# An accumulating transfer for one weight sum, spaced output pieces, early copies of z and start loads from another queue

## The chip, the cores and the metric

One core of a Trainium2 chip runs the kernel; there are no other cores in the program. The metric is device time in microseconds (us) of one execution. Engines are named as in the profile: PE (TensorE), PEld (its weight loads), DVE (VectorE), ACT (ScalarE), POOL (GpSimd), SP (SyncE, which issues most of the transfers). Each engine works through its own instructions in order.

## The reference, cut to what matters

Sixteen learned tokens are put ahead of 512 rows of x, and two layers follow. In each, one wide projection feeds a gated short convolution and a retention branch of four heads; both outputs are gated, summed, projected and normed.

```python
for l in range(DEPTH):                       # DEPTH = 2, D_MODEL = 1024, T = 528
    xn = _rmsnorm(h, pre_norm_g[l])
    proj = xn @ w_in[l] + b_in[l]            # 1024 x 12288
    c_h, c_b, c_c, c_z, r_q, r_k, r_v, r_z, g_a, g_b = jnp.split(proj, split_at, axis=-1)
    y_a = _short_conv_branch(c_h, c_b, c_c, c_z, conv_w[l], conv_b[l], w_conv_out[l])
    y_b = _retention_branch(r_q, r_k, r_v, r_z, ret_gn_g[l], w_ret_out[l])
    y = jax.nn.sigmoid(g_a) * y_a + jax.nn.sigmoid(g_b) * y_b
    y = y @ w_o[l]
    h = h + _rmsnorm(y, post_norm_g[l])
return h[:, N_META:]
```

The convolution branch is `gb * (conv_b + taps of gc * h) * silu(z) @ w_out`. The retention branch rotates q and k, forms decayed scores, multiplies v with them, norms each head's output, multiplies by `silu(z)` and ends in `@ w_out` (four heads of 512 columns).

## The kernel before

Everything is float32. Each matrix is split into a high part (ACT's cast to fp32r) and a low part (DVE's subtraction), by `split`, L139 to L141, and a product takes three matmul passes: high by high, low by high, high by low. Token positions lie along the free axis, 264 to a matmul in the first layer and about 256 to 264 in the second.

The projection goes in blocks of 256 columns, 86 of them as a `Group` (L288). A group treats its 1024 x 256 weight block as 2 x 2 blocks B11, B12, B21, B22 and computes the product with seven block products in place of eight (Winograd's form), each `mul` of 12 matmuls; Xh and Xl hold the blocks A11, A12, A22 of the input and four sums S1 to S4. The weight side needs sums of blocks too. `Group.load` (L299 to L306) fetches three raw tiles of 128 x 1024 by SP: j = 0 with w_0 in the first half and w_1 in the second, j = 1 with w_3 in the second, j = 2 with w_2 in the first and w_1 in the second. The halves of 512 columns are separate transfers of 256 KB. `halves(j)` then adds the first half onto the second (L311, DVE, for j = 0 and for j = 2; for j = 2 this is B22 + B12) and splits the tile (L140 ACT, L141 DVE). `sums` forms two further sums on DVE (L318 from the second half of tile 0 and the first half of tile 2; L319), and `last` splits the fourth tile.

`run` (L331 to L368) issues the seven products into the banks pb, pc and pa. After the first product ACT copies the bank, with the bias, into the shared bank pa (L339), onto which a later product accumulates; `put` evicts the others by ACT (L329). The last product is kept back (`end`) and is issued within the next unit of work.

The order of work is set by three things. `later(delay, fn)` puts small steps into a queue of ticks, and `tick` comes after each product. `load` and `prep` queue transfers and splits, and `pump` issues them as raw slots (six, NSRC) and split pairs (four, NPAIR) come free. The tile scheduler then places the instructions of each engine in a fixed order, and steps under `tc.high_priority()` are preferred in it.

The places that the change touches:

- `conv_group` (L549 to L604) makes the four groups of a convolution block. The last head's four output pieces, `RetOut` (L526; its matmuls are L248), are added with the second convolution block (L938 to L942): two after its third group and two after its fourth. Each piece multiplies that head's normed outputs `yr` with a weight pair and adds onto YB (L546). The blocks 2 and 3 follow (`add_conv`).
- At the start SP issues, in turn, pieces of x (L996) and of the weights of the first K and Q blocks (L1000). ACT's queue has gpre's transfer (L120), an activation table load and the write to `ident` (L981); then come the first prescales and casts, and PE's first projection matmuls (L672).
- The first projections run before the norm's factor R is known. `raw_out` (L1032) copies their results from the banks, and `with_r` (L1035 multiply on DVE, L1036 activation on ACT) applies R and the bias later; for the four tiles of z the activation is Silu (L1073), ahead of the splits of A11, A12, A22 (L1076).
- POOL runs a few memsets of `Slo` (L872) and the `pow` of each norm (L379).

Of the kernel before, what the change touches and what calls it, by code (L numbers as in the profile page):

```python
# [14 lines left out]
AF = mybir.ActivationFunctionType  # L15
ALU = mybir.AluOpType
# [40 lines left out]
def trunk(ctx: ExitStack, tc: tile.TileContext, xT, w_in, binT, w_co, w_ro, w_o, gpre, gpost,  # L57
# [230 lines left out]
    class Group:  # L288
# [10 lines left out]
        def load(self, j, w):  # L299

            t = self.raw[j] = src()
            if j == 1:
                nc.sync.dma_start(t[:, 512:], w[:, 3, :])
                return
            nc.sync.dma_start(t[:, 0:512], w[:, j, :])
            nc.sync.dma_start(t[:, 512:], w[:, 1, :])  # L306

        def halves(self, j):
            if j != 1:
                r = self.raw[j]  # L310
                nc.vector.tensor_tensor(r[:, 512:], r[:, 512:], r[:, 0:512], op=ALU.add)  # L311
# [238 lines left out]
    def conv_group(l, i2, res):  # L550
# [44 lines left out]
        def c_b(ts):  # L595
# [3 lines left out]
            for s in range(2):  # L599
                later(s, lambda s=s: product(s))  # L600
                later(1 + s, lambda s=s: res.append(halves_of(cs, ts[s])))

        return [Group(l, C_H + i2 * 256, I_CONV[l], c_h), Group(l, C_C + i2 * 256, I_CONV[l], c_c),
                Group(l, C_Z + i2 * 256, I_Q[l], c_z, AF.Silu), Group(l, C_B + i2 * 256, I_Q[l], c_b)]  # L604

# [222 lines left out]
    for l in range(DEPTH):  # L828
# [96 lines left out]
        for h in range(1, H):  # L925
# [9 lines left out]
            for b in range(2):  # L935
                add(Group(l, R_Z + h * DV + b * 256, I_Q[l],
                          lambda ts, d=d, h=h, l=l, yr=yrs[h]: z_done(ts, d, h, l, yr), AF.Silu))
        for n, g in enumerate(conv_group(l, 1, conv)):  # L938
            add(g)
            if n >= 2:  # L940
                for q in (2 * n - 4, 2 * n - 3):
                    add(RetOut(l, H - 1, q), yrs[H - 1])  # L942
        add_conv(2)
        add_conv(3)

# [49 lines left out]
    for ks in (slice(0, 1), slice(1, 2), slice(2, 4), slice(4, 6), slice(6, 8)):  # L995
# [3 lines left out]
        for g, c in enumerate((R_K, R_Q)):  # L999
            nc.sync.dma_start(entry[g][j]["raw"].rearrange("p (n k c) -> p n k c", n=2, k=4)[:, :, kk, :],  # L1000
                              w_in[0, c // 256][:, 2 * j:2 * j + 2, :].rearrange("p n (k c) -> p n k c", k=4)[:, :, kk, :])
    for k in range(KD):
# [28 lines left out]
    def raw_out(d, o, m):  # L1031
        nc.scalar.copy(d, o)  # L1032

# [37 lines left out]
    zt = hd["z"][0].ts + hd["z"][1].ts  # L1071
    for n in range(4):
        with_r(zt[n], R_Z // P + n, AF.Silu)  # L1073
    for b, half, j in ((A11, 0, 0), (A12, 0, 4), (A22, 1, 4)):
        for kk in range(0, 4, 2):
            split(Xh[:, b, kk:kk + 2], Xl[:, b, kk:kk + 2], YH[:, j + kk:j + kk + 2, half, :])  # L1076
    later(14, lambda: z_done(zt, jobs[0][0]["hd"], 0, 0, jobs[0]["yrs"][0], (), 13, 8))

# [236 lines left out]
```

## Time and profile before

| | us |
|---|---|
| median of 3 runs | 1537.32 (1536.90 to 1538.46) |
| the profiled execution | 1536.42 |
| its span | 1534.3 |
| PE busy | 1522.3 (99%) |
| PEld busy | 1478.8 (96%) |
| DVE busy | 1172.6 (76%) |
| ACT busy | 916.0 (60%) |
| POOL busy | 27.1 (2%) |
| mean granted clock of PE | 0.999 |

The span is the profile's own time from the first to the last instruction; the execution's time has 2.1 us around it. Busy time of PE is modelled at the ends of matmuls, so neighbouring matmuls overlap in it: in a steady stretch starts are 0.12 us apart and each matmul shows as 0.28 us. A loss is best read from the distance of two starts. Idle time of an engine other than PE costs nothing by itself; it matters where PE waits for that engine.

### The profile page before, as it was taken

The page shows a single profiled execution, that of the slowest core. Times are in us where ns is not written, and L with a number is a line of the kernel's source. Part 1 is how long each engine was busy: PE and PEld are TensorE (multiplying, and loading weights), DVE is VectorE, ACT ScalarE, POOL GpSimd, SP SyncE. Part 2 cuts the span into 40 slices and gives each one's busy share as a digit, 9 for nine tenths or more (in the row PEclk, how much of TensorE's full clock was granted, in tenths as well). Part 3 has the DMA queues.
Part 4 walks back from the last instruction along what each step waited for, and adds up shares of the span by engine and source line. Part 5 has one row for each costly group of instructions (what it writes and reads, how often), then busy time and mean ns, then how long its engine had stood idle before and what let it go on. Part 6 is the DMA issues. An engine that isn't in the chain of part 4 may idle for free.

```text
span 1534.3 us, 29328 instructions
## 1 busy us (share of the span) xinstructions
PE 1522.3 (99%) x11738; PEld 1478.8 (96%) x11738; DVE 1172.6 (76%) x1712; ACT 916.0 (60%) x1772; POOL 27.1 (2%) x31
## 2 busy tenths in 40 slices
PE   9999999999999999999999999999999999999998
PEld 9999999999999999999999999998999999999986
DVE  6998786886877789857379887869779678897642
ACT  7685665565465476646347766655655655676531
POOL 0000000000000000000000000000000000000000
PEclk9999999999999999999999999999999999999999
DMA  8132333232222333435332333332322233434431
GB/s 274 58 124 95 114 108 105 90 119 89 103 98 95 112 125 128 141 131 179 106 105 70 129 99 114 107 111 96 117 91 104 97 110 111 138 131 145 137 99 55
DMA packets 86905, 174.90 MB, mean 114 GB/s; under 512 B 11377, under 2 KB 15985, under 8 KB 86769
## 3 DMA queue, kind: packets, MB, share of 16 engines
q1 hardware_dynamic: 86624, 173.03, 33.1%
q8 instruction: 92, 1.51, 0.4%
q14 instruction: 45, 0.36, 0.1%
q10 hardware_dynamic: 144, 0.01, 0.0%
HBM read 168.74 MB, written 4.26 MB: 113 GB/s over the span
## 4 chain that ended last, share of the span: by engine, by line
PE 93%; DVE 4%; ACT 2%; issue 1%; DMA 1%; DVEq 0%; POOLq 0%; ACTq 0%
PE pb L283 31%; PE pp L248 18%; PE pc L283 15%; PE pa L283 8%; PE pp L672 6%; PE pp L486 5%; PE pb L672 2%; PE pp L1177 2%; PE pp L425 2%; PE pp L454 1%; PE pp L388 1%; DVE wlo L141 1%; ACT whi L140 1%; PE pp L374 1%; DVE Xl L141 0%
## 5 line engine op out<-in xcount | busy, mean ns | idle before, releaser
L140 ACT CAST whi<-raw 128x1024 fp32r<-128x1024 f32 (+2 forms) x356 | 341.5, 967 | 224.1 <-PE pp L248 59.5
L141 DVE TENSOR_TENSOR wlo<-raw,whi 128x1024 fp32r<-128x1024 f32 (+2 forms) x356 | 395.9, 1119 | 101.9 <-ACT whi L140 100.8
L283 PE MATMUL pb<-Xh,whi 128*128 128x264 f32 (+2 forms) x1032 | 296.6, 287 | 3.1 <-ACT pa L339 1.6
L283 PE MATMUL pb<-Xh,wlo 128*128 128x264 f32 (+2 forms) x1032 | 292.0, 283 | 0.0
L283 PE MATMUL pb<-Xl,whi 128*128 128x264 f32 (+2 forms) x1032 | 291.8, 283 | 0.0
L248 PE MATMUL pp<-r,whi 128*128 128x264 f32 (+1 forms) x1152 | 244.7, 321 | 0.0
L283 PEld LDWEIGHTS pb<-Xh,whi 128*128 128x128 f32 x1032 | 194.3, 188 | 4.8 <-ACT pa L339 2.2
L283 PE MATMUL pc<-Xh,whi 128*128 128x264 f32 (+2 forms) x688 | 196.9, 286 | 0.7 <-ACT f L329 0.7
L283 PEld LDWEIGHTS pb<-Xl,whi 128*128 128x128 f32 x1032 | 194.3, 188 | 0.7
L283 PE MATMUL pc<-Xl,whi 128*128 128x264 f32 (+2 forms) x688 | 194.9, 283 | 0.0
L283 PE MATMUL pc<-Xh,wlo 128*128 128x264 f32 (+2 forms) x688 | 194.6, 283 | 0.0
L283 PEld LDWEIGHTS pb<-Xh,wlo 128*128 128x128 f32 x1032 | 194.2, 188 | 0.0
L248 PEld LDWEIGHTS pp<-r,whi 128*128 128x128 f32 x1152 | 177.1, 188 | 15.9 <-DVE YB L546 0.4
L248 PE MATMUL pp<-r,wlo 128*128 128x264 f32 (+1 forms) x576 | 153.1, 321 | 0.0
L311 DVE TENSOR_TENSOR raw<-raw 128x512 f32<-128x512 f32 x172 | 117.6, 687 | 42.0 <-DMA raw<-in_w_in 41.3
L283 PEld LDWEIGHTS pc<-Xh,whi 128*128 128x128 f32 x688 | 129.5, 188 | 1.4 <-ACT f L329 1.4
L283 PEld LDWEIGHTS pc<-Xl,whi 128*128 128x128 f32 x688 | 129.5, 188 | 0.0
L283 PEld LDWEIGHTS pc<-Xh,wlo 128*128 128x128 f32 x688 | 129.3, 188 | 0.0
L248 PEld LDWEIGHTS pp<-r,wlo 128*128 128x128 f32 x576 | 95.4, 188 | 8.3
L283 PE MATMUL pa<-Xh,whi 128*128 128x264 f32 (+2 forms) x344 | 98.6, 287 | 0.0
L283 PE MATMUL pb<-Xh,whd 128*128 128x264 f32 (+2 forms) x344 | 97.6, 284 | 0.2 <-ACT f L329 0.2
L283 PE MATMUL pb<-Xh,wld 128*128 128x264 f32 (+2 forms) x344 | 97.5, 283 | 0.0
(286 smaller groups left out, 3226.0 us busy)
## 6 DMA issues: line engine op xcount, KB each, us to landing
raw<-in_w_in SPq DMA_DIRECT2D x436, 256.0 KB, 2.9
raw<-in_w_ro SPq DMA_DIRECT2D x32, 512.0 KB, 3.3
raw<-in_w_in SPq DMA_DIRECT2D x16, 512.0 KB, 5.2
raw<-in_w_co SPq DMA_DIRECT2D x16, 512.0 KB, 3.3
raw<-in_w_o SPq DMA_DIRECT2D x16, 512.0 KB, 3.9
Dsb<-in_decay SPq DMA_DIRECT2D x8, 520.0 KB, 4.6
h1d<-f SPq DMA_DIRECT2D x8, 264.0 KB, 4.6
f<-h1d SPq DMA_DIRECT2D x8, 264.0 KB, 4.9
```

Of the source, the lines that this page charges most:

```text
L140: nc.scalar.copy(dst_hi, src)
L141: nc.vector.tensor_tensor(dst_lo, src, dst_hi.bitcast(F32), op=ALU.subtract)
L248: nc.tensor.matmul(banks[i][:, 0:cols.n], wt(k)[:, msl], xs(k)[:, sl], start=(k == 0 and a == 0), stop=(k == nk - 1 and a == 2),)
L283: nc.tensor.matmul(o[:, 0:n], wt[:, k, :], xs[:, blk, k, HALF - n:], start=(first and k == 0 and a == 0), stop=(k == 3 and a == 2), skip_g ...
L311: nc.vector.tensor_tensor(r[:, 512:], r[:, 512:], r[:, 0:512], op=ALU.add)
L374: nc.tensor.matmul(pp[0:sc, 0, c:c + 1], sums[:, t0 + c * sc:t0 + (c + 1) * sc], ones_d[:, 0:1], start=True, stop=True)
L388: nc.tensor.matmul(pp[:, c // per, (c % per) * sc:(c % per + 1) * sc], y[:, c:c + 1].to_broadcast([sc, P]), ident[0:sc, 0:sc], start=True, ...
L425: nc.tensor.matmul(pp[0:kn, n + i, 0:cols.n], k[dt][x][:, k0:k0 + kn] if j < 4 else k8[:, dt * 2 + x, :], q[dt][y][:, sl], start=(dt == 0 ...
L454: nc.tensor.transpose(pp[0:kn, b, v * P:(v + 1) * P], vt[v][:, k0:k0 + kn] if j < 4 else v8[:, v, :], ident)
L486: nc.tensor.matmul(pp[:, b, lo_ - banks[b][0]:hi_ - banks[b][0]], V[j][x][0:kn, v * P:(v + 1) * P], S[0:kn, SOFF[j] + lo_ - q0:SOFF[j] + h ...
L672: nc.tensor.matmul(o, wt(k), xs[:, i0:], start=(k == 0 and a == 0), stop=(k == KD - 1 and a == 2))
L1177: nc.tensor.matmul(o, x[:, xs], wo[k][half][w], start=(k == 0 and a == 0), stop=(k == KD - 1 and a == 2))
```

## The change

Four things change. For j = 2 a group now loads w_2 into both halves with one broadcasting transfer of 512 KB on SP, and then w_1 is added onto the second half by a transfer that accumulates, issued by POOL; the DVE addition for j = 2 goes (86 of 172). The last head's four output pieces are placed one after each of the groups 2 to 5 of the twelve that follow, and `conv_group` yields its groups one at a time. The first two K and Q weight pieces are issued by ACT. `raw_out` gets high priority, and the multiply and Silu of the four z tiles are put off to ticks 4, 6, 8 and 10, behind the splits of A11, A12 and A22.

```diff
@@ -302,11 +302,15 @@
             if j == 1:
                 nc.sync.dma_start(t[:, 512:], w[:, 3, :])
                 return
+            if j:
+                nc.sync.dma_start(t.rearrange("p (a c) -> p a c", a=2), w[:, j:j + 1, :].to_broadcast([P, 2, 512]))
+                nc.gpsimd.dma_start(t[:, 512:], w[:, 1, :], accum_op=ALU.add)
+                return
             nc.sync.dma_start(t[:, 0:512], w[:, j, :])
             nc.sync.dma_start(t[:, 512:], w[:, 1, :])
 
         def halves(self, j):
-            if j != 1:
+            if j == 0:
                 r = self.raw[j]
                 nc.vector.tensor_tensor(r[:, 512:], r[:, 512:], r[:, 0:512], op=ALU.add)
             self.w[j] = wtile("whi"), wtile("wlo")
@@ -600,8 +604,9 @@
                 later(s, lambda s=s: product(s))
                 later(1 + s, lambda s=s: res.append(halves_of(cs, ts[s])))
 
-        return [Group(l, C_H + i2 * 256, I_CONV[l], c_h), Group(l, C_C + i2 * 256, I_CONV[l], c_c),
-                Group(l, C_Z + i2 * 256, I_Q[l], c_z, AF.Silu), Group(l, C_B + i2 * 256, I_Q[l], c_b)]
+        for col, i0, cb, act in ((C_H, I_CONV, c_h, AF.Identity), (C_C, I_CONV, c_c, AF.Identity),
+                                 (C_Z, I_Q, c_z, AF.Silu), (C_B, I_Q, c_b, AF.Identity)):
+            yield Group(l, col + i2 * 256, i0[l], cb, act)
 
     class ConvOut:
 
@@ -935,13 +940,10 @@
             for b in range(2):
                 add(Group(l, R_Z + h * DV + b * 256, I_Q[l],
                           lambda ts, d=d, h=h, l=l, yr=yrs[h]: z_done(ts, d, h, l, yr), AF.Silu))
-        for n, g in enumerate(conv_group(l, 1, conv)):
+        for n, g in enumerate(g for i2 in (1, 2, 3) for g in conv_group(l, i2, conv)):
             add(g)
-            if n >= 2:
-                for q in (2 * n - 4, 2 * n - 3):
-                    add(RetOut(l, H - 1, q), yrs[H - 1])
-        add_conv(2)
-        add_conv(3)
+            if 2 <= n <= 5:
+                add(RetOut(l, H - 1, n - 2), yrs[H - 1])
 
         def gate_b(ts, b, l=l):
             cs = slice(QCOLS[l].t0, T)
@@ -997,8 +999,9 @@
         j = ks.start // 4
         kk = slice(ks.start - 4 * j, ks.stop - 4 * j)
         for g, c in enumerate((R_K, R_Q)):
-            nc.sync.dma_start(entry[g][j]["raw"].rearrange("p (n k c) -> p n k c", n=2, k=4)[:, :, kk, :],
-                              w_in[0, c // 256][:, 2 * j:2 * j + 2, :].rearrange("p n (k c) -> p n k c", k=4)[:, :, kk, :])
+            q = nc.scalar if ks.stop <= 2 else nc.sync
+            q.dma_start(entry[g][j]["raw"].rearrange("p (n k c) -> p n k c", n=2, k=4)[:, :, kk, :],
+                        w_in[0, c // 256][:, 2 * j:2 * j + 2, :].rearrange("p n (k c) -> p n k c", k=4)[:, :, kk, :])
     for k in range(KD):
         for half in range(2):
             prescale(0, k, half, YH[:, k, half, :])
@@ -1029,7 +1032,8 @@
     R = fslot()
 
     def raw_out(d, o, m):
-        nc.scalar.copy(d, o)
+        with tc.high_priority():
+            nc.scalar.copy(d, o)
 
     def with_r(t, m, func=AF.Identity):
         nc.vector.tensor_tensor(t, t, R, op=ALU.mult)
@@ -1069,11 +1073,11 @@
     hd["z"][1].run(0, raw_out)
     hd["z"][1].run(1, raw_out)
     zt = hd["z"][0].ts + hd["z"][1].ts
-    for n in range(4):
-        with_r(zt[n], R_Z // P + n, AF.Silu)
     for b, half, j in ((A11, 0, 0), (A12, 0, 4), (A22, 1, 4)):
         for kk in range(0, 4, 2):
             split(Xh[:, b, kk:kk + 2], Xl[:, b, kk:kk + 2], YH[:, j + kk:j + kk + 2, half, :])
+    for n in range(4):
+        later(4 + 2 * n, lambda n=n: with_r(zt[n], R_Z // P + n, AF.Silu))
     later(14, lambda: z_done(zt, jobs[0][0]["hd"], 0, 0, jobs[0]["yrs"][0], (), 13, 8))
 
     for l in range(DEPTH):
```

ACT at the start of the program, before (raw_135 is K's raw tile, raw_137 Q's):

```order
L120 DMA gpre_sb<-in_gpre 128x16
L981 ACT_TABLE_LOAD
L981 ACTIVATE ident<-ones_d 128x1
L658 ACTIVATE Xh<-YB,gpre_sb 128x264
L658 ACTIVATE r_121<-YB,gpre_sb 128x264
L140 CAST whi_129<-raw_135 128x128
```

and now:

```order
L120 DMA gpre_sb<-in_gpre 128x16
L983 ACT_TABLE_LOAD
L983 ACTIVATE ident<-ones_d 128x1
L1003 DMA raw_135<-in_w_in 128x2x128
L1003 DMA raw_137<-in_w_in 128x2x128
L1003 DMA raw_135<-in_w_in 128x2x128
L1003 DMA raw_137<-in_w_in 128x2x128
L663 ACTIVATE Xh<-YB,gpre_sb 128x264
L663 ACTIVATE r_121<-YB,gpre_sb 128x264
L140 CAST whi_129<-raw_135 128x128
```

Four transfers stand between the write to `ident` and the first prescale.

ACT near the end of the first projections, before (f_932, f_1004, f_1068 and f_1141 are the z tiles, L1032 the copies from the banks):

```order
L1032 COPY f_1068<-pp_1007 128x264 x2
L140 CAST Xh<-YB 128x528 x2
L140 CAST whi_1137<-raw_677 128x1024
L1036 ACT_TABLE_LOAD
L1036 ACTIVATE f_932<-f_932,bin_92 128x528
L1036 ACTIVATE f_1004<-f_1004,bin_92 128x528
L140 CAST Xh<-YB 128x528
L1032 COPY f_1141<-pb_1071 128x264
L329 ACTIVATE f_1166<-pc_1168 128x264
L1032 COPY f_1141<-pb_1072 128x264
L140 CAST Xh<-YB 128x528
```

and now, with the copies at L1036, the Silus at L1040 and the copy into pa at L343:

```order
L140 CAST whi_1136<-raw_677 128x1024
L140 CAST Xh<-YB 128x528
L1036 COPY f_1140<-pb_1070 128x264
L1036 COPY f_1140<-pb_1071 128x264
L140 CAST Xh<-YB 128x528 x2
L333 ACTIVATE f_1157<-pc_1159 128x264
L140 CAST Xh<-YB 128x528
L448 CAST Shi_903<-f_1133 80x528
L1040 ACT_TABLE_LOAD
L1040 ACTIVATE f_932<-f_932,bin_92 128x528
L343 ACTIVATE pa_104<-pb_1158,bin_92 128x264
L140 CAST whi_1208<-raw_838 128x1024
```

All copies of z now stand ahead of the table load, and one Silu follows it directly, ahead of the copy into pa.

DVE a little later, where the second and third groups' weights are prepared, before (raw_840 is a j = 2 tile, raw_999 a j = 0 tile):

```order
L141 TENSOR_TENSOR wlo_1218<-raw_838,whi_1217 128x1024
L436 TENSOR_TENSOR f_1273<-pp_1260,Dsb 128x192
L436 TENSOR_TENSOR f_1275<-pp_1260,Dsb 128x64
L311 TENSOR_TENSOR raw_840<-raw_840 128x512
L141 TENSOR_TENSOR wld_1287<-t_1214,whd_1286 128x512
L445 TENSOR_TENSOR Slo_904<-f_1273,Shi_903 128x192
L445 TENSOR_TENSOR Slo_904<-f_1275,Shi_903 64x64
L311 TENSOR_TENSOR raw_999<-raw_999 128x512
L141 TENSOR_TENSOR wlo_1280<-raw_840,whi_1279 128x1024
```

and now (the multiplies by R of two z tiles are L1039):

```order
L141 TENSOR_TENSOR wlo_1272<-raw_840,whi_1271 128x1024
L141 TENSOR_TENSOR wld_1279<-t_1205,whd_1278 128x512
L440 TENSOR_TENSOR f_1264<-pp_1251,Dsb 128x192
L440 TENSOR_TENSOR f_1266<-pp_1251,Dsb 128x64
L1039 TENSOR_TENSOR f_1004<-f_1004,f_457 128x528
L449 TENSOR_TENSOR Slo_904<-f_1264,Shi_903 128x192
L449 TENSOR_TENSOR Slo_904<-f_1266,Shi_903 64x64
L315 TENSOR_TENSOR raw_999<-raw_999 128x512
L1039 TENSOR_TENSOR f_1067<-f_1067,f_457 128x528
```

The addition on raw_840 is gone, the one on raw_999 remains, and two multiplies of z tiles stand where none did.

PE where the first output piece of the last head begins in the first layer, before (pp is a piece's bank, pb and pc the banks of groups, r the split yr tiles):

```order
L283 MATMUL pb_6363<-Xh,wlo_6055 128x264
L248 MATMUL pp_6227<-r_6144,whi_6219 128x264 x2
L248 MATMUL pp_6227<-r_6145,whi_6219 128x264 x2
L248 MATMUL pp_6266<-r_6144,whi_6219 128x264 x2
L248 MATMUL pp_6266<-r_6145,whi_6219 128x264 x2
L283 MATMUL pb_6363<-Xh,whi_6054 128x264
L283 MATMUL pb_6363<-Xl,whi_6054 128x264
L283 MATMUL pb_6363<-Xh,wlo_6055 128x264
L283 MATMUL pb_6363<-Xh,whi_6093 128x264
```

and now:

```order
L248 MATMUL pp_6202<-r_6168,whi_6029 128x264 x2
L248 MATMUL pp_6241<-r_6114,whi_6029 128x264 x2
L248 MATMUL pp_6241<-r_6115,whi_6029 128x264 x2
L248 MATMUL pp_6241<-r_6114,wlo_6030 128x264 x2
L248 MATMUL pp_6241<-r_6136,whi_6029 128x264 x2
L248 MATMUL pp_6202<-r_6169,whi_6029 128x264 x2
L248 MATMUL pp_6202<-r_6168,wlo_6030 128x264 x2
L283 MATMUL pb_6039<-Xh,whd_5988 128x264
L283 MATMUL pb_6039<-Xl,whd_5988 128x264
L248 MATMUL pp_6202<-r_6185,whi_6029 128x264 x2
L283 MATMUL pb_6039<-Xh,wld_5989 128x264
```

Before, parts of both halves of the piece stand inside the first product of a new group (into pb_6363); now they run together behind the sixth product of the previous group and mix with its last one (pb_6039 with whd).

On POOL 86 transfers are added, in order with its memsets and pow instructions; all matmuls are as they were, 11613 on PE in both.

## Rows read from the trace of the kernel before

**Rows 1.** The page: busy times, then busy tenths of 40 slices (38.4 us each).

```profile
PE 1522.3 (99%) x11738; PEld 1478.8 (96%) x11738; DVE 1172.6 (76%) x1712; ACT 916.0 (60%) x1772; POOL 27.1 (2%) x31
...
DVE  6998786886877789857379887869779678897642
...
DMA  8132333232222333435332333332322233434431
```

**Rows 2.** PE's waits, whole span: line, waited for, us, times, longest.

```profile
PE pb L283 <- ACT pa L339: 1.6, 3, 0.6
PE pb L283 <- ACT f L1032: 1.4, 1, 1.4
```

**Rows 3.** Busy time of each engine by window: us, PE, PEld, DVE, ACT, POOL.

```profile
40.00:60.00 20.00, 20.00 (x166) 20.00 (x166) 20.00 (x33) 10.48 (x20) 0.00 (x0) 1.00 0.18 59
...
80.00:100.00 20.00, 17.69 (x138) 16.84 (x137) 18.72 (x32) 17.93 (x38) 0.00 (x0) 1.00 0.34 117
...
480.00:500.00 20.00, 19.39 (x156) 18.90 (x155) 17.73 (x28) 10.05 (x17) 0.00 (x0) 1.00 0.22 76
...
1240.00:1260.00 20.00, 19.40 (x115) 16.76 (x114) 17.35 (x25) 8.77 (x15) 0.00 (x0) 1.00 0.24 79
1500.00:1534.00 34.00, 28.31 (x131) 22.84 (x129) 11.19 (x20) 7.45 (x20) 2.19 (x4) 0.97 0.17 62
```

**Rows 4.** The page's groups: L311, busy, mean ns of one, idle before.

```profile
L311 DVE TENSOR_TENSOR raw<-raw 128x512 f32<-128x512 f32 x172 | 117.6, 687 | 42.0 <-DMA raw<-in_w_in 41.3
```

**Rows 5.** Timeline of PE around 83 us: start, length, what, idle before.

```profile
81.50 0.57 PE L425 MATMUL pp<-r,r 128*128 128x448 f32 x2
83.51 0.39 PE L283 MATMUL pb<-Xh,whi 128*128 128x264 f32 x1 [1.44 <-ACT f L1032]
```

**Rows 6.** Timeline of ACT around 80 us.

```profile
80.00 1.28 ACT L1036 ACT_TABLE_LOAD   x1
...
83.09 0.37 ACT L1032 COPY f<-pb 128x264 f32<-128x264 f32 x1
```

**Rows 7.** Timeline of the start, several engines.

```profile
1.17 0.94 SPq L1000 DMA_DIRECT2D raw<-in_w_in  x2
...
2.46 0.20 ACT L981 ACTIVATE ident<-ones_d 128x1 f32<-128x1 f32 x1
...
4.00 0.51 ACT L658 ACTIVATE Xh<-YB,gpre_sb 128x264 fp32r<-128x264 f32 x1 [1.34 <-DMA gpre_sb<-in_gpre]
...
4.83 0.48 ACT L140 CAST whi<-raw 128x128 fp32r<-128x128 f32 x2
...
5.17 0.59 PE L672 MATMUL pp<-Xh,whi 128*128 128x264 f32 x1
```

**Rows 8.** Timeline of PE near the last head's output pieces.

```profile
486.37 0.28 PE L283 MATMUL pb<-Xl,whi 128*128 128x264 f32 x1
486.49 0.28 PE L283 MATMUL pb<-Xh,wlo 128*128 128x264 f32 x1
487.38 0.39 PE L283 MATMUL pb<-Xh,whi 128*128 128x264 f32 x1 [0.61 <-ACT pa L339]
```

**Rows 9.** Timeline: one j = 2 tile, its issue, its sum, its cast.

```profile
560.02 0.33 SPq L305 DMA_DIRECT2D raw<-in_w_in  x1
...
565.13 0.69 DVE L318 TENSOR_TENSOR raw<-raw,raw 128x512 f32<-128x512 f32 x1 [2.37 <-DMA raw<-in_w_in]
...
577.67 1.06 ACT L140 CAST whi<-raw 128x1024 fp32r<-128x1024 f32 x1 [0.94 <-DMA raw<-in_w_in]
```

**Rows 10.** The page's DMA issues: KB each, median us to landing.

```profile
raw<-in_w_in SPq DMA_DIRECT2D x436, 256.0 KB, 2.9
raw<-in_w_ro SPq DMA_DIRECT2D x32, 512.0 KB, 3.3
raw<-in_w_in SPq DMA_DIRECT2D x16, 512.0 KB, 5.2
```

**Rows 11.** Timeline of POOL, one pow of a norm.

```profile
141.09 2.80 POOL L379 TENSOR_TENSOR ny<-nv,mhalf 88x6 f32<-88x6 f32 x1 [11.25 <-DVE nv L378]
```


## The prediction

> **What bounds the kernel now.** I read the page's busy times and slices first. PE is busy for 99% of the span [rows 1]. The changed kernel issues the same matmuls, so only time in which PE stands still can be won: 1534.3 − 1522.3 = 12.0 us. Next come the windows and the list of PE's waits, to place those 12 us. Some are fixed: the start, where PE's first projection matmul comes at 5.17 us after warm-up work [rows 7], and the end, where the last norm and store run without it (34.00 − 28.31 = 5.7 us from 1500 on [rows 3]). In between lie few stalls. The stretch from 80 to 100 us holds 20.00 − 17.69 = 2.31 us of idle PE, those from 480 and from 1240 us 0.61 and 0.60 [rows 3]. The named waits are for L1032's eviction (1.4 us, one wait) and for L339's copy into pa (1.6 in three) [rows 2]. That list is short of the loss, because a matmul after a stop also starts the next ones late: from 486.49 to 487.38 us two starts lie 0.89 apart, where 0.12 is usual (486.37 to 486.49), so 0.77 is lost where the row names 0.61 [rows 8]. So I put the stops at up to 1.35 times their rows: 80 to 98 us at up to 3.1, and the two pa stretches at up to 1.3 each with the small gaps behind them. What is left of the 12.0 us is 12.0 − 5.7 − 2.3 − 1.2 = 2.8, about 1 of it at the start, 1.5 to 2 scattered. Some 7 us is all that any reordering could give back.
>
> VectorE is at 76% over the span, yet full from 40 to 60 us, where PE idles not at all, and at 9 in five later slices [rows 1, 3]. So the 86 additions that the change takes from VectorE are worth something only where VectorE is late for PE: in the stretch from 38 to 98 us.
>
> **The additions.** Half of L311's 172 additions go: 86 × 687 ns = 59 us of VectorE [rows 4]. Outside the early stretch nothing waits for them: the addition runs between the landing and ScalarE's cast of the same tile, and that cast has room. One case: issue at 560.02, the first half landed at about 565.1 (L318 starts as the DMA releases it), cast at 577.67, so 12.5 us later [rows 9]. Part of the freed time is no gain at all, since VectorE stood idle before L311 for 41.3 us, waiting for the same transfers [rows 4]. Their price outside 38 to 98 us I take as 0, with the cover named: those 12 us.
>
> What replaces them costs elsewhere. One 512 KB transfer stands for the first 256 KB one, and L318 waits for all of it. The nearest rows are 2.9 us for 256 KB and 3.3 to 5.2 for 512 KB [rows 10], so the sums start 0.4 to 2.3 us later where they wait on the DMA; I take 0.8. This is hidden by the sums' own distance to the matmuls that use them, and where VectorE is full the 0.69 us that the addition gave up behind it pays for it. The queues carry 86 × 256 KB = 22 MB more, an eighth of what they carry now, and the slices show them 5 tenths busy at most behind the start [rows 1]. The accumulating transfer starts when the broadcast has landed, in GpSimd's order, behind a pow of up to 2.8 us in a few places [rows 11]. No row shows such a transfer. From below it is bounded by 2.9 us, a plain one, and from above by two 512 KB ones in a row, 10.4; I take 5, nearer to the plain one, since only the second operand is new. All three are under 12, so: 0. If the cover were gone, each microsecond beyond it would fall on PE in every group where VectorE runs close behind: by the slices at 9 outside the start, 5 of 38.4 us, with about 3.5 groups in each (a group is 84 matmuls of 0.12 us, 10.2 us), that is some 18 groups.
>
> **80 to 98 us, −2.2.** At 80.00 us ScalarE loads an activation table for 1.28 us and then runs two Silus, and L1032's copies stand behind it, from 83.09 on [rows 6]; PE, which had issued its last matmul after 81.50, starts again at 83.51 [rows 5]. In the changed order these copies of all four z tiles stand before the table load, with priority, and the multiplies and Silus of the z tiles come 4 to 10 ticks later. The first stop (1.4 by its row, 1.6 by starts) should go. The two later ones (0.6 each by starts) are ScalarE and VectorE still catching up; two j = 2 additions leave that stretch (1.4 us), but two multiplies now enter it. Against it: the table load and the first Silu now stand right ahead of a copy into pa (L343), so some of the stop can come back there. The ends are 0 and −3.1; I take −2.2, nearer to the sum of the rows (2.31).
>
> **Start, +0.8.** Four weight pieces move from SP's queue to ScalarE's, behind gpre, the table load and ident. The first K piece was issued at 1.17 us and had landed by 4.83, when its cast starts [rows 7], within 3.7; it can now be issued at 2.66, when ident ends, so it lands by 6.3 at the latest. The four issues at 0.47 each (0.94 for two on SP) also hold ScalarE until about 4.5, so the first prescale, at 4.00 before, starts then. The first projection matmul follows the cast by 0.34, so 5.17 becomes 5.7 to 6.6. For it speaks that SP is free of four issues, 1.9 us, and the later pieces of x and of the weights come earlier. The start is a race for bandwidth, so some of the loss is recovered. Ends: −0.3 (all later pieces on time and the small gaps behind 5.17 closed) and +1.5 (the whole delay of the issue, nothing recovered); I take +0.8, above the middle. It carries through, because VectorE is full from 38.8 us on and has nothing to absorb it with. The Trainium skill's page "DMA: Bandwidth & Descriptors", section "Issuing engines are not separate DMA queues", says that issuing from several engines saves only the issuing time; this agrees with the 1.9 us, and without them the term would be its upper end.
>
> **Last head's output pieces, −1.2.** Today all four pieces load and run after the second and third group of the second conv block, two and two; the planner mixes them into other products, and a copy into pa then has PE waiting (0.77 at 487 us) [rows 8]. Afterwards one piece follows each of four groups. Each piece is still 24 (or 12) matmuls of PE's own; the weight pair of each is prepared at an easier pace. It could all go, −2.6 for two layers, or only move, 0, and a wait on yr tiles can come, since the first piece stands no later than before. I take the middle, −1.2.
>
> **Other stalls, −0.4** of 1.5 to 2, between 0 and −1.5: VectorE has less to do, but no row shows that these wait for it alone.
>
> **Sum.** −2.2 + 0.8 − 1.2 − 0.4 = −3.0. The profiled execution took 1536.42 (its span is 1534.3, with 2.1 around it) and lies 0.9 under the median of the runs, 1537.32; the median is the base: 1537.3 − 3.0 = 1534.3. The limits of what counts as a difference, 0.2% or 3.07 us (about what a measurement of this kernel can tell from no change), are 1534.25 and 1540.4, so the forecast stands on the edge of "faster".
>
> **Rivals.** *Given back.* The stop at 83.5 us moves to the copy into pa behind the table load, and the start pays 1.4: −0.8 − 0.5 + 1.4 = about 0, 1537.4. For it: VectorE remains full from 40 to 98 us, and the freed additions were largely idle waiting for the DMA anyway. Against it: the first stop's cause is plainly the order on ScalarE.
>
> *The accumulate is late (slower).* Transfer and queue together take more than the 12 us between the landing and the cast. With 0.4 us beyond it, 18 groups × 0.4 = 7 us: 1537.3 − 3 + 7 = 1541, and 1 us beyond it 1552. It decides from about 12 us after the broadcast's landing. For it: no row shows a transfer of GpSimd's, and VectorE is busy there. Against it: even 10.4 us fits. The Trainium skill's page "SBUF — State Buffer", section "Who interferes with whom", states that GpSimd shares a port pair with VectorE and that a transfer which seems stalled by VectorE was one whose descriptors GpSimd writes; by this rule the accumulate would be the slow part. It exempts two-input tensor_tensor from that effect. By the fit in "DMA: Bandwidth & Descriptors", section "Anatomy of one DMA", 256 KB take about 2.6 us (an estimate), which leaves the sum as it is. No row shows either. In rows: VectorE's longest instruction there lasts 1.2 us, so being held up by several would still fit.
>
> *All stops vanish.* The 3.1, 2.6 and 1.8, with the start at +0.3: 1537.3 − 7.2 = 1530.1.
>
> **Chances.** Forecast, 1531.5 to 1536: 0.60, of which 0.35 under the limit and 0.25 above; given back, 1536 to 1538.5: 0.15; late accumulate, over 1540.4: 0.13; all vanish: 0.12. Faster 0.47, same 0.40, slower 0.13. The range 1530 to 1541 leaves out half of the third rival's cases on one side (0.06) and most of the late accumulate's (0.11) on the other.
>
> **What would show it.** In the changed profile: no wait of PE for the raw copy and a window from 80 to 100 us with under 1 us idle (against it: a wait on pa after the table load); first projection matmul between 5.7 and 6.6 us; no wait on pa near 487 and 1244 us; VectorE's busy time down by 59 us with PE's unchanged; the accumulating transfers landing within 3 to 8 us and no cast of a j = 2 tile having PE behind it. Casts waiting on GpSimd's queue with PE idle behind them would prove the forecast wrong, and so would new waits on the sums in the full stretches.

## The result, and the profile after

The changed kernel takes 1546.94 us (median of 5 runs, 1542.28 to 1549.94) against 1536.90 (5 runs, 1536.27 to 1538.46): a ratio of 1.0059, 95% interval 1.0048 to 1.0071. It is about 9 us slower. Its profiled execution took 1549.94, the longest of the five, with a span of 1548.1.

The page of the changed kernel: busy times, the transfer queues (packets, MB, share of the time of the 16 transfer engines), the chain of work that ended last, and the issues (KB each, median us to landing). These lines answer to [rows 1] and [rows 10]:

```profile
PE 1526.7 (99%) x11738; PEld 1482.9 (96%) x11738; DVE 1123.7 (73%) x1626; ACT 914.9 (59%) x1772; POOL 102.4 (7%) x117
...
q1 hardware_dynamic: 84160, 172.50, 34.0%
q0 software_dynamic: 12384, 22.55, 9.0%
...
PE 85%; DVE 6%; DMA 4%; ACT 3%; issue 2%; SPq 0%; DVEq 0%; ACTq 0%; POOLq 0%
...
raw<-in_w_in SPq DMA_DIRECT2D x264, 256.0 KB, 3.3
raw<-in_w_in SPq DMA_DIRECT2D x102, 512.0 KB, 3.4
raw<-in_w_in POOLq DMA_DIRECT2D x86, 256.0 KB, 4.0
```

DVE did get 49 us back (1172.6 to 1123.7; 59 were forecast). PE runs 11738 matmuls in both traces (the 11613 given earlier is not their count), but its idle time rose from 12.0 to 21.4 us, its busy time by 4.4, and transfers now stand in the chain with 4%, where they had 1%. The accumulating queue q0 moves 22.55 MB and takes 9.0% of the engines' time, q1 172.50 MB and 34.0%: twice the time for each byte. PE's waits show new lines where [rows 2] had L1032 and L339:

```profile
PE pp L458 <- DVE r L471: 6.8, 5, 2.4
PE pc L283 <- ACT f L333: 2.9, 3, 1.6
PE pb L677 <- ACT whi L140: 1.5, 1, 1.5
...
PE pb L283 <- ACT pa L343: 0.3, 1, 0.3
```

L458 is the transposes of v (L454 before), L471 the DVE instruction that frees their bank, L333 the eviction of a product (L329 before), L677 a projection matmul of the start. The copy into pa is nearly gone from the list, as meant. The windows, columns as in [rows 3], place the loss:

```profile
0.00:20.00 20.00, 17.01 (x109) 16.70 (x110) 12.23 (x40) 14.55 (x42) 0.84 (x7) 0.91 0.93 304
80.00:100.00 20.00, 18.77 (x147) 17.84 (x146) 19.51 (x31) 17.87 (x38) 1.75 (x2) 1.00 0.51 159
480.00:500.00 20.00, 20.00 (x166) 20.00 (x166) 19.19 (x30) 12.58 (x23) 0.94 (x1) 1.00 0.36 107
...
860.00:880.00 20.00, 16.89 (x130) 16.48 (x129) 13.90 (x23) 14.21 (x33) 1.74 (x2) 0.91 0.42 118
1200.00:1220.00 20.00, 17.84 (x138) 17.63 (x137) 12.53 (x19) 14.72 (x31) 1.48 (x2) 0.91 0.38 108
```

From 80 to 100 us PE idles 1.23 us where it was 2.31, and from 480 to 500 not at all. But in the first 20 us (3.0 us idle, 1.2 before) and at two places of the second layer 2 to 3 us are lost to idling, with the granted clock down to 0.91 in each. Since PE runs nearly the same order of matmuls in both, the two traces can be laid side by side: I took the start of the n-th matmul in each and subtracted. The changed kernel is 2.8 us late by 23 us, has won back 1.1 by 104, wins 1.3 near 490, loses 1.4 near 614 and 0.9 near 710, then 5.1 between 825 and 887, 2.0 up to 1132, 3.9 between 1192 and 1230, and wins 1.3 near 1250. These add to 12.4 us; the rest of the 13.8 by which the spans differ are small drifts between them.

One of those places, near 1207 us, in the timelines of POOL, SP, DVE and PE. The first row is the same addition in the kernel before:

```profile
1193.72 0.69 DVE L311 TENSOR_TENSOR raw<-raw 128x512 f32<-128x512 f32 x1 [1.94 <-DMA raw<-in_w_in]
```
```profile
1199.72 0.89 POOL L307 DMA_DIRECT2D raw<-in_w_in  x1 [11.93 <-DVE r L471]
...
1201.07 0.33 SPq L309 DMA_DIRECT2D raw<-in_w_in  x1
1201.45 0.50 SPq L310 DMA_DIRECT2D raw<-in_w_in  x1
...
1207.98 0.69 DVE L315 TENSOR_TENSOR raw<-raw 128x512 f32<-128x512 f32 x1 [4.91 <-DMA raw<-in_w_in]
1208.59 0.74 DVE L471 SCALAR_TENSOR_TENSOR r<-pp,vs,r 128x512 fp32r<-128x512 f32 x1
...
1206.95 0.28 PE L283 MATMUL pa<-Xh,wlo 128*128 128x256 f32 x1
1209.39 0.66 PE L458 MATMUL pp<-ident,f 128*128 128x128 f32 x4 [2.16 <-DVE r L471]
...
1210.87 0.41 PE L283 MATMUL pc<-Xh,whi 128*128 128x256 f32 x1
1211.08 0.41 PE L283 MATMUL pc<-Xl,whi 128*128 128x256 f32 x1
```

POOL issues the accumulation of one group. 1.35 us later SP issues the two j = 0 halves of the next. The second of them lands after 6.4 us, where it took 3.5 at this place before and 3.1 in the median. DVE stands at its addition for 4.91 us instead of 1.94 (L315, the j = 0 addition that was kept), and behind it in DVE's order stands L471, which has nothing to do with weights but frees the bank that PE needs. PE starts nothing from 1206.95 to 1209.39, and afterwards its matmuls start 0.21 apart instead of 0.12 for 3.4 us.

### The profile page after: what moved, and what is told of

Same layout as the page of the kernel before. It is cut to its first block, busy times and chain, and to the rows that moved or that the text cites. A ratio compares the mean times of both kernels' runs of the same rounds, so it can differ in the third digit from the quotient of the medians.

```text
span 1548.1 us, 29362 instructions
## 1 busy us (share of the span) xinstructions
PE 1526.7 (99%) x11738; PEld 1482.9 (96%) x11738; DVE 1123.7 (73%) x1626; ACT 914.9 (59%) x1772; POOL 102.4 (7%) x117
## 3 DMA queue, kind: packets, MB, share of 16 engines
q1 hardware_dynamic: 84160, 172.50, 34.0%
q0 software_dynamic: 12384, 22.55, 9.0%
## 4 chain that ended last, share of the span: by engine, by line
PE 85%; DVE 6%; DMA 4%; ACT 3%; issue 2%; SPq 0%; DVEq 0%; ACTq 0%; POOLq 0%
PE pb L283 27%; PE pp L248 16%; PE pc L283 14%; PE pa L283 7%; PE pp L677 6%; PE pp L490 5%; DMA raw<-in_w_in 4%; PE pb L677 3%; PE pp L1181 2%; DVE wlo L141 2%; PE pp L429 2%; ACT whi L140 1%; PE pp L458 1%; PE pp L392 1%; PE pp L378 1%
## 5 line engine op out<-in xcount | busy, mean ns | idle before, releaser
L307 POOL DMA_DIRECT2D raw<-in_w_in x86 | 75.6, 879 | 1085.4 <-DMA raw<-in_w_in 551.6
L315 DVE TENSOR_TENSOR raw<-raw 128x512 f32<-128x512 f32 x86 | 59.2, 688 | 85.2 <-DMA raw<-in_w_in 84.9
L322 DVE TENSOR_TENSOR raw<-raw,raw 128x512 f32<-128x512 f32 x86 | 59.2, 689 | 59.0 <-DMA raw<-in_w_in 58.8
```

The source lines that it names most:

```text
L307: nc.gpsimd.dma_start(t[:, 512:], w[:, 1, :], accum_op=ALU.add)
L322: nc.vector.tensor_tensor(b[:, 0:512], a[:, 512:], c[:, 0:512], op=ALU.add)
```

## The experiments

The parts are taken one by one first, then the accumulation is taken apart. The time of before is given from the same chip, since each set has its own.

### e1: everything but the accumulation

```diff
 changed kernel, Group.load and halves
-            if j:
-                nc.sync.dma_start(... w[:, j:j + 1, :].to_broadcast([P, 2, 512]))
-                nc.gpsimd.dma_start(t[:, 512:], w[:, 1, :], accum_op=ALU.add)
-                return
-            if j == 0:
+            if j != 1:
```

> All of the change except the accumulating transfer: j = 2 is loaded in two plain halves and added on DVE as before. Collision theory (the accumulating transfer delays the next group's j = 0 halves, DVE stands in order before their addition, and the evictions behind it let PE wait): the waits of PE for L471's line and for L333's line near 614, 866, 1105 and 1207 us go, only the start's loss remains (about 0.4 + 1.6 us of idle and about 1.7 at half clock) against 2 to 3 won elsewhere, so 1537 to 1538. Order theory (the new order of pieces and copies makes these waits, whatever loads the weights): the waits stay, 1543 or more.

Measured: 1537.56 against 1537.05, ratio 1.0003 (0.9994 to 1.0012). No wait for L471's counterpart is left in PE's list. The order theory falls: without the accumulation the new order of pieces and copies makes none of these waits.

### e2: the accumulation alone

The edit is the first hunk of the diff of the change (`Group.load` and `halves`) on the kernel before.

> The kernel before with the accumulating transfer alone. Collision theory: 1543 to 1547, with DVE idle before the j = 0 addition (after: 85 us, before: 41 us for both additions) and waits of PE of 1 us and more where v is transposed. Order theory: 1536 to 1538, no such waits. As I predicted at first: 1537 or less.

Measured: 1545.55 against 1537.05, ratio 1.0051 (1.0039 to 1.0064). PE waits at the transposes and DVE before the kept addition, as after:

```profile
PE pp L458 <- DVE r L471: 5.2, 5, 2.3
```
```profile
DVE raw L322 <- DMA raw<-in_w_in: 60.2, 46, 3.4
DVE raw L315 <- DMA raw<-in_w_in: 68.8, 38, 4.4
```

In the kernel before, both additions together waited 41.3 us [rows 4]; now half of them wait 68.8. The accumulation is the loss. Side by side with before, this trace loses 5.0 us between 825 and 887 us and 1.5 between 1192 and 1230, at the same places. Nor are the j = 0 halves merely issued later. Measured from the same point of PE's work in both traces, they are issued at the same time as before (0.0 us later in the median) and land 0.2 later in the median; at the two places above they are issued 0.4 and 0.1 later and land 2.2 and 2.4 later.

### e3: the start alone

```diff
-            nc.sync.dma_start(entry[g][j]["raw"]...
+            q = nc.scalar if ks.stop <= 2 else nc.sync
+            q.dma_start(entry[g][j]["raw"]...
```

> The kernel before with the first K and Q pieces issued by ACT alone. From the changed kernel's trace, where PE stood still for 0.4 us more before its first projection matmul, for 1.6 us a little later and ran at half clock for 3.4 us behind that: 1540 to 1541 if all of this carries through to the end; 1538 if the clock's part or the later pieces are made up before 40 us; 1537 if nothing carries through.

Measured: 1541.32 against 1537.05 (1538.78 to 1543.38 in 10 runs), ratio 1.0027 (1.0018 to 1.0036). Its profiled execution is the fastest of the ten (1538.78). It is 2.2 us late by 23 us and 2.3 at the end, so this part carries through; where the slower runs lose the other 2 us of the median, no trace shows. PE's first matmul comes in time and then one stop follows, for the cast of a Q piece:

```profile
5.25 0.59 PE L672 MATMUL pp<-Xh,whi 128*128 128x264 f32 x1 [0.20 <-ACT whi L140]
...
7.60 0.30 ACT L140 CAST whi<-raw 128x128 fp32r<-128x128 f32 x1 [2.20 <-DMA raw<-in_w_in]
...
7.95 0.39 PE L672 MATMUL pb<-Xh,whi 128*128 128x264 f32 x1 [1.68 <-ACT whi L140]
```

### e4, e10, e12: output pieces and z

e4 has the hunks of `conv_group`, of the last head's pieces, of `raw_out` and of z; e10 the last two alone, e12 the first two alone.

> The kernel before with the spaced output pieces, the early copies of z and the late Silus of z, and neither of the two changes of transfers. If the gains that I counted are real (1.2 for the pieces, 1.1 to 2.2 between 80 and 98 us): 1533.5 to 1535. If they only move: 1536 to 1537. If the pieces' or the Silus' new places cost in layer 2 by themselves: above 1538.

> The early copies of z and the late Silus alone. The fourth run, with the spaced pieces as well, was 2.8 us faster. By the stops counted in its trace (about 1.1 in all between 80 and 98 us instead of 2.8) this part gives 1.7: 1535.0 to 1536. If the pieces gave all of it: 1537. If this part gave all: 1534.2.

> The spaced output pieces alone. Laying the traces side by side, the pieces gave 1.1 us near 490 and 1.3 near 1250 in the fourth run, and the copies and Silus of z gave 1.7 near 90, of which 1.4 was lost again between 130 and 165. If that holds: 1534 to 1535, no slower than with both parts (1534.2 in its own set), and the pieces are all of the gain. If the two parts only help together: 1536 to 1537.

Measured: e4 1534.20 against 1537.05, ratio 0.9982 (0.9974 to 0.9991); e10 1538.12 against 1536.58, ratio 1.0012 (1.0004 to 1.0021); e12 1534.44 against 1537.09, ratio 0.9982 (0.9973 to 0.9991). The pieces carry the whole gain; e10 missed every number that I had set for it. Windows of e4:

```profile
80.00:100.00 20.00, 19.42 (x152) 18.49 (x151) 19.56 (x33) 17.55 (x38) 0.00 (x0) 1.00 0.38 123
120.00:140.00 20.00, 19.08 (x159) 18.87 (x158) 13.18 (x22) 9.75 (x20) 0.15 (x1) 1.00 0.19 62
480.00:500.00 20.00, 20.00 (x167) 20.00 (x166) 18.45 (x28) 11.70 (x21) 0.00 (x0) 1.00 0.30 100
```

From 80 to 100 us idle PE falls from 2.31 [rows 3] to 0.58, the gain that was looked for. Between 120 and 140, where PE never stopped before, 0.92 us come back at once:

```profile
128.38 0.69 DVE L311 TENSOR_TENSOR raw<-raw 128x512 f32<-128x512 f32 x1 [1.38 <-DMA raw<-in_w_in]
```
```profile
134.76 0.39 PE L283 MATMUL pc<-Xh,whi 128*128 128x264 f32 x1 [0.92 <-ACT f L329]
```

DVE stands before an addition for its transfer, the group's sum and the Silu of ACT follow it, and the eviction that PE needs stands behind that Silu. Side by side, e4 gains 1.7 us by 104 and gives 1.4 back by 165. e10 gains 1.7 and gives back 1.4, and it is 0.75 late from the start, whose instructions are the same as before. That 0.75 and some small losses behind 700 us make e10's excess; why they came in all of its runs (1537.93 to 1539.03) stays open.

### e5, e6, e7, e8: what in the accumulation costs

e5 drops the addition for j = 2 and changes no transfer. It, e6 and e8 leave B22 out of the second half of that tile. e6 has the broadcast and then w_1 plain, both by SP. e7 only lets POOL issue w_1 of j = 2, plain, with the additions kept. e8 is e2 with a plain transfer in place of the accumulating one:

```diff
-                nc.gpsimd.dma_start(t[:, 512:], w[:, 1, :], accum_op=ALU.add)
+                nc.gpsimd.dma_start(t[:, 512:], w[:, 1, :])
```

> The kernel before with the addition for j = 2 left out and nothing in its place, so the second half of that tile holds B12 alone and the products made with it lack B22: what 86 fewer additions on DVE are worth by themselves, the most that the accumulating transfer could win. As I put it in the prediction (worth something between 38 and 98 us alone): 1535 to 1537. If DVE were late for PE elsewhere too: 1533 or less.

> The transfers' size alone: SP loads w_2 twice (512 KB), then w_1 over the second half by a plain transfer, also from SP; no addition for j = 2 (its second half holds B12 alone). If 22 MB more and the wait of SP between the two transfers are what costs: 1541 or more. If the size is not the matter: like the kernel without that addition, within 1.5 us. SP waits for the broadcast to land before it issues the second, and that holds the next group's loads behind it by some 3 us, so a loss here may also be SP's waiting; SP's waits would tell.

> The queue alone: the kernel before, all additions kept, sizes as before, and only w_1 of j = 2 issued by POOL as a plain transfer of 256 KB. If it is the descriptors or the packets of POOL's queue that get in the way of SP's transfers: 1540 or more, with packets of POOL's queue at well over 84 ns and SP's j = 0 halves at 4 us where they overlap. If it is the accumulation alone: 1537 to 1538, packets at about 84 ns.

> The transfers as in the accumulating version, each in its place and at its size (broadcast on SP, w_1 by POOL after it has landed), but the second one plain; the addition for j = 2 is in neither, so the second half holds B12 alone. If the accumulation itself (read and write of the destination, 178 ns a packet where a plain one takes 84) is the cause: 1536 to 1538.5, against 1545.5 for the accumulating one. If size, queue and place are: 1543 or more.

Measured, all against 1537.02:

| | us | ratio (95%) |
|---|---|---|
| e5, 86 additions less | 1535.44 | 0.9989 (0.9980 to 0.9998) |
| e8, same transfers, plain | 1537.88 | 1.0006 (0.9997 to 1.0015) |
| e6, both by SP | 1540.34 | 1.0023 (1.0014 to 1.0031) |
| e7, POOL's queue, additions kept | 1543.06 | 1.0035 (1.0023 to 1.0048) |
| e2, accumulating (its own set) | 1545.55 | 1.0051 (1.0039 to 1.0064) |

The additions are worth 1.7 us (0.0011 of 1537). The larger transfers and POOL's queue cost 2.6 us (e8 against e5), and the accumulation itself 7 more (1.0051 − 1.0006; the two come from different sets, each taken against its own time of before). The queue lines say what is different, e8's first, then e2's:

```profile
q0 software_dynamic: 6880, 22.55, 4.5%
```
```profile
q0 software_dynamic: 12384, 22.55, 9.0%
```

The same bytes come in 1.8 times the packets and take twice the engines' time. In the median an accumulating packet of 2048 bytes took 178 ns in q0 of the changed kernel and a plain one of that size 84 in q1; e8's packets in q0 hold 4096 bytes and took 159. The second j = 0 halves (L310) land after 3.3 us in the median and 4.8 at most in e8, 3.5 and 5.9 in e2, 3.7 and 6.4 in the changed kernel. There the 60 of 86 that overlap an accumulation land after 4.06, the other 26 after 3.21 (worked out from each issue and landing). It is the late ones that grow in number: 3 of 86 took over 4.5 us in e8, 14 in e2, 19 in the changed kernel. That the longer use of the shared engines is how the accumulation delays them is the likely reading; no run shows it apart.

e6 fell between my two numbers. SP stood there 182.7 us, in 81 waits, for the broadcast before it issued the second transfer, with the next loads behind it, so size and waiting are not told apart. e7 met its first number (1540 or more), but not the reasons given with it: its packets took 159 ns for 4096 bytes, as plain ones do in q1, and the j = 0 halves that overlap POOL's transfers landed after 3.6 us in the median, not 4. It is slower than e8 for another reason. Its additions on DVE must wait for POOL's transfer, where in e8 only ACT's cast does: DVE waits 53.4 us before L311 in e7 against 41.3, and 15.1 of them for POOL's transfers, where the same halves from SP cost 3.5 before. The longest of these waits, 2.61 us at 598 us, is followed by a late load of SP's (1.6 us later at 601 us, by PE's work) and by PE's longest stop, 2.19 us by starts at 613 us. That it is this and nothing else was not tried.

### e9, e11, e13: the accumulation held back

POOL looks at the next raw tile before it issues the accumulation, so it starts when that tile has landed:

```diff
+    def settle(t=None):
+        while late:
+            c, w = late.pop()
+            if t is not None:
+                nc.gpsimd.tensor_tensor(seen, t[:, 511:513], t[:, 511:513], op=ALU.subtract)
+                nc.gpsimd.tensor_tensor(c[:, 512:514], c[:, 512:514], seen, op=ALU.add)
+            nc.gpsimd.dma_start(c[:, 512:], w[:, 1, :], accum_op=ALU.add)
```

e11 adds e4's parts. e13 looks at columns 510 and 511 instead, the half that SP then loads last.

> The accumulating transfer alone, as in the second run, but held back: POOL first reads two columns of the next raw tile that SP loads (in 70 of 86 groups), so the accumulation starts when that tile, mostly the next group's j = 0, has landed. Size, queue and accumulation are unchanged, only the time at which it runs. If it costs because it runs beside the j = 0 halves: DVE's wait before the j = 0 addition falls from 69 us to about 45, the waits of PE for L471's line go, and the time is 1537 to 1540. If the accumulation costs wherever it runs: 1543 or more, as before (1545.5). If it now comes too late for the cast of its own tile: above 1546, with ACT waiting for POOL's transfers.

> The spaced pieces, the early copies and late Silus, and the accumulating transfer held back as in the first run of this set; the start as before. If the parts add up and holding back takes the accumulation's cost down to nothing: 1533 to 1535, no slower than without the accumulation (1534.2). If holding back removes only part: 1536 to 1541, and the version without it stays the best.

> The accumulation held back again, without the fault of the earlier attempt, in which DVE's addition on the next j = 0 tile had to wait for POOL's look at its second half (29.6 us of DVE waits): POOL now looks at the first half, which SP loads last. If running beside the j = 0 halves is what costs: under 1541. If the accumulation then only falls beside the next j = 1 and j = 2 transfers, as DVE's longer wait before the sums in that attempt (89 us against 59) suggests: 1546 or more, with that wait still above 80.

Measured: e9 1554.13 against 1536.58, ratio 1.0116 (1.0100 to 1.0131); e11 1550.00, ratio 1.0092 (1.0079 to 1.0106); e13 1549.69 against 1537.09, ratio 1.0095 (1.0064 to 1.0126). For e11 both of my numbers were wrong; e9 is above 1546, but not for the reason given, since the waits that grew are DVE's. DVE's waits in e9, then in e13 (L337 is the first sum, L330 the addition):

```profile
DVE raw L337 <- DMA raw<-in_w_in: 89.0, 50, 3.9
DVE raw L330 <- POOL seen L204: 29.6, 26, 2.3
DVE raw L330 <- DMA raw<-in_w_in: 24.5, 14, 3.9
```
```profile
DVE raw L337 <- DMA raw<-in_w_in: 84.1, 49, 4.1
DVE raw L330 <- DMA raw<-in_w_in: 49.4, 39, 4.0
```

e9 made a wait of its own: the addition may not overwrite what POOL still looks at. In e13 that is gone, and the wait before the addition is down to 49.4 from e2's 68.8, as the collision theory had it; PE waits no more at the transposes. But the time rose: the wait before the sums, which stand for the broadcast, is 84.1 against 60.2, and PE now stops for evictions (L348, 8.0 us in five waits). The collision has moved to the next transfer that DVE waits for: in e13 38 of the 86 broadcasts overlap an accumulation and land after 4.01 us in the median, the other 48 after 3.39, while in e2 a single one overlaps. Of the j = 0 halves 20 now overlap one, where 62 did in e2. My number for this case (under 1541) was wrong and the other (1546 or more, that wait above 80) right.

### e14: the accumulation in the first layer only

```diff
+            if j and not self.l:
+                nc.sync.dma_start(...)
+                nc.gpsimd.dma_start(t[:, 512:], w[:, 1, :], accum_op=ALU.add)
+                return
```

The addition for j = 2 stays on DVE in the second layer.

> The accumulating transfer in the first layer only, additions on DVE in the second. By the side-by-side reading of the traces, 8 of its 10 us come in the second layer, at the transposes of v (about 5 us near 866, 0.6, 0.8 and 1.5 at the later heads) and little in the first: 1537.5 to 1539. If it costs evenly wherever it runs, for every transfer beside it: about half, 1541.

Measured: 1536.92 against 1537.09, ratio 1.0000 (0.9991 to 1.0009), just under my first number. DVE waits more there too (59.0 us before the additions, 67.8 before the sums), yet PE's idle time is 12.4 us against 12.0. So most of the loss is the second layer's, where an eviction for PE stands behind the waiting addition (866 and 1207 us); in e2's trace 7.7 of 9.5 us come behind 820 us. The first layer is not free in every execution: e14's profiled one, its second slowest (1538.62), loses 2.3 us there in small pieces. The accumulation in the second layer alone was not run.

## Why the prediction was wrong

**What bounds the kernel** was read rightly, and used on one side only. PE's stops were counted as all that could be won; that a later landing makes new ones, wherever PE's evictions stand behind DVE's wait, was priced for the accumulated tile alone.

**The additions: the step that failed.** Their worth was right: e5 gives 1.7 us, and 1.4 of it between 64 and 104 us, the one stretch that I named. What replaces them I set to 0, because "All three are under 12". That is true of the accumulated tile: its transfers landed after 3.6 to 7.9 us, 4.0 in the median (I took 5), and no cast of it held PE. It was the wrong tile. The transfers beside it paid. The queues that I called 5 tenths busy at most were averages over slices of 38.4 us, while 60 of the 86 second j = 0 halves are in flight together with an accumulation (issued between 3.9 us before it and 4.4 behind it). The wait of 41.3 us before L311, which I read as freed time that is no gain, was the warning: an engine that already waits at a landing 37 times, with other engines' evictions behind it, has no cover at all for a later landing. The term is about +8 (e2), not 0, with the 1.7 us of the dropped additions already in it.

The rival *the accumulate is late* had the sign and a range that holds the time (1541 to 1552), but by luck: its mechanism did not occur, since no landing took 12 us. The Trainium skill's page "SBUF — State Buffer", section "Who interferes with whom", says of a transfer which seems held up by VectorE that GpSimd was kept from writing its descriptors, and exempts tensor_tensor. POOL's 86 issues took 0.86 to 1.06 us each, so none was held up, which agrees with the exemption. The Trainium skill's page "DMA: Bandwidth & Descriptors", section "Anatomy of one DMA", has a fit for transfers that GpSimd issues, which gives 2.6 us for 256 KB (an estimate). The accumulating ones took 4.0, the plain ones in the same place 3.1 (e8).

**Start: +0.8 was +4.1** (e3, of which its trace places 2.2 at the start and the changed kernel's 2.8), beyond the upper end. Two readings failed. ACT's transfers don't wait for the table load and `ident`, as I read the order; they are issued beside them, at 1.25 us. And the delay is not of the first K piece (the first projection matmul comes at 5.52 us, not at 5.7 to 6.6) but of the Q piece:

```profile
1.25 1.43 ACTq L1003 DMA_DIRECT2D raw<-in_w_in  x3
...
2.48 0.20 ACT L983 ACTIVATE ident<-ones_d 128x1 f32<-128x1 f32 x1
...
5.52 0.40 PE L677 MATMUL pp<-Xh,whi 128*128 128x264 f32 x1 [0.46 <-ACT whi L140]
...
7.41 0.30 ACT L140 CAST whi<-raw 128x128 fp32r<-128x128 f32 x1 [1.74 <-DMA raw<-in_w_in]
...
7.76 0.39 PE L677 MATMUL pb<-Xh,whi 128*128 128x264 f32 x1 [1.48 <-ACT whi L140]
```

SP no longer sends small weight pieces between x's: it issues three pieces of x by 2.06 us, and the four pieces from ACT took 5.9 us to land in the median, against 4.0 from SP. The first Q piece is issued when it was before (1.67 us, 1.64 before), but the third piece of x is now issued ahead of it (1.64 instead of 2.15), and it lands at 7.39 instead of 5.44. By these rows SP's own order had made the pieces land when they were needed; I credited SP's 1.9 freed us as a help, and they were the harm. No run holds x's third piece back, so this reading is argued.

**80 to 98 us: −2.2 was −1.7, and then nearly 0.** The copies moved as described (idle PE 2.31 to 0.58 in e4), and the table load with a Silu now stands ahead of the copy into pa, at a price of 0.3 us only:

```profile
86.30 1.28 ACT L1040 ACT_TABLE_LOAD   x1
87.60 0.74 ACT L1040 ACTIVATE f<-f,bin 128x528 f32<-128x528 f32 x1
88.24 0.43 ACT L343 ACTIVATE pa<-pb,bin 128x264 f32<-128x264 f32 x1
```

What I left out is the next thing that is late: PE 1.7 us earlier meets the same landings 30 to 60 us on, and 1.4 are lost again.

**The pieces: −1.2 was −2.7** (e12), the far end of my range; both waits for pa went, and no wait for yr tiles came. The trace agrees: it wins 1.3 near 490 us and 1.3 near 1250. **Other stalls: −0.4** came to nothing that can be told apart.

By the ratios the parts add up: 7.8 (e2) + 4.1 (e3) − 2.8 (e4) = 9.1 us, and the whole is 0.0059 × 1537 = 9.1.

The spaced pieces alone (e12), or with z (e4), beat both kernels: 1534.2 to 1534.4, 0.18% under before.

## What to carry to other kernels

Before a transfer is made longer or moved to another queue, look not at the slack of its own tile but at every transfer beside it whose landing an in-order engine waits for, and at what stands behind that wait for the engine that bounds the kernel. An idle time "until DMA" on an engine that is not the bottleneck is a place where the next microsecond of landing goes through. And a gain at one place has to be followed to the next landing downstream before it is counted.

## What the runs showed of the hardware

Transfers that accumulate into SBUF took twice the engines' time of plain ones of the same size from the same queue (9.0% of the span against 4.5%, e2 and e8): 178 ns in the median for 2048 bytes, where plain ones went in packets of 4096 bytes at 159.

A stop of PE can cost more than its length. After stops of 2.4 and 2.7 us by starts (near 1207 and 866 us) and after the two at the start, the granted clock fell to the lower of its two levels (1.2 instead of 2.4 GHz) for 3.4 us, which leaves 0.91 in the mean of the 20 us windows, and matmuls started 0.21 us apart. It fell in the same way after the stop of 2.19 us in e7 (the windows columns as above):

```profile
600.00:620.00 20.00, 18.09 (x136) 17.88 (x135) 17.29 (x24) 13.04 (x22) 1.07 (x2) 0.91 0.32 106
```

The kernel before, whose longest stop after the start is 1.44 us [rows 5], shows it nowhere in the middle of its span. But not every stop of this length does it: after 2.43 us by starts near 575 us in e13 and 2.40 near 870 in e9 the granted clock stayed at the upper level. Each fall adds about 1.7 us (half of 3.4), so the three make some 5 of the 13.8 in the profiled execution.
